# A hybrid mixer block on one core: scores over 128 rows, another order of the branches, weights of the last stage a tile ahead

## The chip, the core and the metric

The kernel runs on one core of a Trainium2 chip. TensorE (PE in the rows; PEld is its weight load) multiplies matrices, VectorE (DVE) works on whole tiles, ScalarE (ACT) computes functions and copies, and SyncE (SP) issues most transfers; each engine takes its instructions in the order in which the program holds them. The metric is the device time of one execution in microseconds (us), lower is better.

## What is computed

One block over 1024 tokens of 1024 features. Four branches of width 256 are computed from a normalized input, each is multiplied by its own matrix and gated, and their sum goes through an output matrix; a gated FFN and a last gated projection follow.

```python
h = rmsnorm(x, g_mix)
(a_b, a_c, a_x, q, k, v, s_u, s_v, c_val, c_gate) = split(h @ w_in, 10)   # 256 features each
y_a = a_b * causal_dwconv(a_c * a_x, conv_a)          # short convolution, 3 taps
y_b = dilated_attention(q, k, v)                      # 4 heads of 64, three window groups in one softmax
y_c = spatial_gating(s_u, s_v, sgu_ln_g, sgu_ln_b, sgu_w, sgu_b)
y_d = conformer_conv(c_val, c_gate, conf_dw, conf_ln_g, conf_ln_b)        # 31 taps
merged = sum(sigmoid(h @ w_merge_gate[br]) * (branches[br] @ w_branch[br]) for br in range(4))
x = x + merged @ w_out
f_gate, f_up = split(rmsnorm(x, g_ffn) @ w_ffn_in, 2)                     # hidden 2816
x = x + (silu(f_gate) * f_up) @ w_ffn_out
x = x + sigmoid(rmsnorm(x, g_ple) @ w_ple_gate) * (p @ w_ple_proj)
return rmsnorm(x, g_final)
```

## The kernel before

Features lie on the 128 partitions, tokens in the free dimension. A product of F32 values is made of three matmuls: each operand is split into a rounded F32R part (`h`, "hi", a ScalarE cast) and the rest (`l`, "lo", a VectorE subtraction), and `mm_k` adds hi·hi, lo·hi and hi·lo. The large square products (branch gates, `gt`; FFN, `fg`/`fo`) use seven block products instead of eight (`pair`); its seven weights `p0` to `p6` are sums of blocks, split like the others.

The program is written as one pass; a scheduler fixes the order on each engine when the program is built, and tile pools decide when a buffer can be taken again: T and M (large tiles), W (raw weights, 3 buffers), WS (2), WP (a hi and a lo pool of 4 each). The stages in time: projections to 99.6 us; attention to 222 us; spatial gating, conformer and short convolution to 320 us; the gates and branches to 717 us; output matrix and FFN to 1449 us; the last stage to the end.

**Attention.** `qk(ct)` makes queries and keys of one column tile of 128 features, two heads of 64. For head h it writes `qs` (query hi in the head's 64 rows, query lo in the other 64) and `kd` (key hi in both halves), so that one matmul over 128 rows gives hi·hi + lo·hi. The third product takes `kl`, the keys' lo parts of both heads in one tile, over the head's 64 rows alone (L396). `attend` loops over 8 blocks of 128 queries and 2 heads, 32 steps in all: the scores `sc` go into one PSUM buffer (L395, L396, in pieces of up to 512 keys, so 48 pairs), VectorE adds the mask and takes the minimum (L400), ScalarE exponentiates (L402), PE transposes (L409), ScalarE copies the transposed block (L410), PE multiplies by the values (L415). Between these PE has projections of other branches (`pj`, `sp`), and VectorE has the 31 taps of the conformer convolution (L332).

**Branches.** For each branch in `ORDER`, `load_parts` reads its output `y` back from DRAM (`yda` to `ydd`, written there by `spill`) and splits it; then for four pairs of column tiles `pair` computes the gates, and the branch's product `br` is gated and added to `mg`. The short convolution (`short_conv`, branch 0) is the last branch that is computed before this loop, in six steps; between its steps `gate_operands` prepares the normalized input for the gates. ScalarE copies partial gate sums out of PSUM (`gt00n<-gt00u`, L580).

**Last stage.** `PIECES` are 768 and 256 tokens; for each output tile m of 8, `pg` is the gate's product (weights `wpg`, 1024 deep) and `pq` the projection's (weights `wpp`, 256 deep). Tiles 4 to 7 of `wpg` are kept split for the second piece, the others are read and split again. Then VectorE scales (L891), ScalarE takes the sigmoid (L892), VectorE multiplies and adds (L893, L895), ScalarE squares for the last norm (L899, L906). The finished first piece is scaled meanwhile by VectorE (L858) and written out. At the end `rsqrt_col` sums the squares (`fin1ss`, PE) and takes a square root on ScalarE (L215).

Of the kernel before, what the change touches and what calls it, by code (L numbers as in the profile page):

```python
# [8 lines left out]
F32 = mybir.dt.float32  # L9
F32R = mybir.dt.float32r  # L10
AF = mybir.ActivationFunctionType
# [12 lines left out]
NEG = 3.0e38  # L24
CHUNKS = ((0, 4), (4, 7))
SINGLE = ((7, 8, 9), (10,))
ORDER = (0, 1, 2, 3)
PIECES = ((0, 768), (768, 256))


# [9 lines left out]
def mixers_kernel(ctx, tc, xT, pT, vec, mask, sgu_ln, sgu_wT, sgu_b, w_in, w_tok, w_gate, w_br, w_out,  # L40
# [27 lines left out]
    def M(name, dt=F32, w=S):  # L68
        return mp.tile([P, w], dt, tag="m", name=name, padded_shape=[P, S], bufs=8)
# [1 line left out]
    def W(name, w=S):  # L71
        return wp.tile([P, w], F32, tag="wr", name=name, padded_shape=[P, S], bufs=3)

    def WS(name, w=512):
        return wp.tile([P, w], F32, tag="sw", name=name, padded_shape=[P, 512], bufs=2)

    def WP(name):
        return (wp.tile([P, 512], F32R, tag="wh", name=name + "h", bufs=4),
# [274 lines left out]

    def qk(ct):

        qs, kd = [], []
        kl = None
        for nm, i in (("q", 6 + ct), ("k", 8 + ct)):
            ps = proj_tile(i)
            t = T(f"{nm}{ct}")  # L360
            if nm == "q":
                nc.vector.scalar_tensor_tensor(t, ps, -(64.0 ** -0.5), rs, ALU.mult, ALU.mult)
                for h in range(2):
                    a, b = slice(h * 64, h * 64 + 64), slice(64 - h * 64, 128 - h * 64)
                    d = M(f"qs{ct}{h}", F32R)
                    nc.scalar.copy(d[a, :], t[a, :])
                    nc.vector.tensor_sub(d[b, :], t[a, :], d[a, :].bitcast(F32))
                    qs.append(d)
            else:
                nc.vector.tensor_mul(t, ps, rs)  # L370
                kl = M(f"kl{ct}", F32R)
                for h in range(2):
                    a, b = slice(h * 64, h * 64 + 64), slice(64 - h * 64, 128 - h * 64)
                    d = M(f"kd{ct}{h}", F32R)
                    nc.scalar.copy(d[a, :], t[a, :])
                    nc.scalar.copy(d[b, :], t[a, :])
                    nc.vector.tensor_sub(kl[a, :], t[a, :], d[a, :].bitcast(F32))
                    kd.append(d)
        return qs, kd, kl

    yb = [T(f"yb{ct}") for ct in range(2)]
# [3 lines left out]
    def attend(ct, qs, kd, kl):  # L385
        for b in range(NB):
            L = (b + 1) * P
            rl = sm.tile([P, 2, 64], F32, tag="rl", name=f"rl{ct}{b}", bufs=2)
            for h in range(2):
                a = slice(h * 64, h * 64 + 64)  # L390
                sc = banks.pools["s"].tile([P, S], F32, tag="s", name=f"sc{ct}{b}{h}", bufs=1)
                q = qs[h][:, b * P:(b + 1) * P]
                for c in range(0, L, 512):
                    n = min(512, L - c)
                    nc.tensor.matmul(sc[:, c:c + n], q, kd[h][:, c:c + n], start=True, stop=False)  # L395
                    nc.tensor.matmul(sc[:, c:c + n], q[a, :], kl[a, c:c + n], start=False, stop=True)  # L396
                pr, pt = prs[h], pts[h]
                nm = sm.tile([P, 1], F32, tag="nm", name=f"nm{ct}{b}{h}")
                ls = sm.tile([P, 1], F32, tag="ls", name=f"ls{ct}{b}{h}")
# [231 lines left out]
        yield  # L631

    for n, _ in enumerate(step for ct in range(2) for step in short_conv(ct)):
        if 1 <= n <= 4:
            gate_operands(n - 1)


    banks.close()
# [145 lines left out]

    ws = {(i, c): load_single(i, c) for i, c in ((SINGLE[0][0], 0), (SINGLE[0][0], S))}
    acts = [single_operands(i) for i in SINGLE[0][:2]]
    for ci, (i0, i1) in enumerate(CHUNKS):
        n = i1 - i0

# [38 lines left out]
        for m in range(0, KD, 2):  # L828
            for k, h, ps, t in pair(f"fo{ci}{m}", raws if m == 0 else load_two(m), n):
                x = x2[m + k][:, h * 512:h * 512 + 512]  # L830
                if ci == 1 and m == 6 and (k, h) == (1, 0):
                    wpg0, wpp0 = load_w("wpg00", w_pg[0]), load_w("wpp00", w_pp[0], 256)
                nc.vector.tensor_add(x, x, t)
                nc.vector.tensor_add(x, ps, x)
                if ci == 1 and m == 6 and ready:
                    i = ready.pop(0)
                    n3.add(i, x2[i])
            ready += [m, m + 1]
            while ci == 1 and m != 4 and ready:
                i = ready.pop(0)  # L840
                n3.add(i, x2[i])
# [3 lines left out]
    banks = Banks(True)  # L845


    kept = {}
    late = []

    def finish(ci, c0, H, acc):
# [8 lines left out]

        return [norm] + [lambda m=m: out(m) for m in range(KD)]

    ORD2 = (4, 5, 6, 7, 0, 1, 2, 3)
    xg = []
    steps = []
    for ci, (c0, H) in enumerate(PIECES):
        acc = T(f"oacc{ci}", F32, H)
        for m in (tuple(range(KD)), ORD2)[ci]:
            if m in kept:
                w = kept[m]  # L870
            elif m >= 4:
                raw = W(f"wpg{m}r")
                nc.sync.dma_start(raw, w_pg[m])
                hi, lo = parts(f"wpg{m}", raw).both
                w = kept[m] = [(hi[:, c:c + P], lo[:, c:c + P]) for c in range(0, S, P)]
            else:
                w = load_w(f"wpg{ci}{m}", w_pg[m]) if ci or m else wpg0
            wq = load_w(f"wpp{ci}{m}", w_pp[m], 256) if ci or m else wpp0
            if H > 512:
                pg, po = G(f"pg{ci}{m}"), G(f"pq{ci}{m}")  # L880
            else:
# [5 lines left out]
                         [(c, min(c + 512, c0 + H)) for c in range(c0, c0 + H, 512)], c0)  # L887
            if ci == m == 0:
                r3 = n3.rstd()
            t = T(f"pt{ci}{m}", F32, H)  # L890
            nc.vector.tensor_mul(t, pg[:, :H], r3[:, c0:c0 + H])  # L891
            nc.scalar.activation(t, t, AF.Sigmoid)  # L892
            nc.vector.tensor_mul(t, t, po[:, :H])  # L893
            xs = x2[m][:, c0:c0 + H]
            nc.vector.tensor_add(xs, xs, t)  # L895
            if m == 4 * ci:
# [111 lines left out]
```

## Time and profile before

| | us |
|---|---|
| median of 3 runs | 1584.57 |
| lowest, highest | 1583.59, 1586.0 |
| profiled execution | 1587.8 |
| span of that execution | 1585.9 |
| PE busy in it | 1565.9 (99%) |
| DVE busy in it | 1186.1 (75%) |
| ACT busy in it | 681.2 (43%) |

The rows come from the profiled execution, which took 3.2 us more than the median; 1.9 us of its time lie outside the span. Its mean granted clock of TensorE was 0.996 of full speed. "Busy" of PE counts overlapping instructions once. In the rows, "idle before" is the engine's idle time just ahead of an instruction, and the arrow names what ended it.

### The profile page before, as it was taken

What the parts mean: (1) busy time and instruction counts of PE and PEld (TensorE: products, weight loads), DVE (VectorE), ACT (ScalarE), POOL (GpSimd) and SP (SyncE); (2) the same over time, 40 slices, a digit from 0 to 9 for tenths busy, and PEclk for the clock granted to TensorE, in tenths of its full rate; (3) what the DMA queues carried; (4) which work ended last, traced back from release to release, by engine and by line L of the source; (5) the groups of instructions that cost most, each with busy time, mean ns of one, the idle gap of its engine ahead of it and who ended that gap; (6) DMA issues with size and microseconds to landing.
All of it is one profiled execution on the core that took longest, in us unless ns stands there. A gap on an engine that the chain in (4) does not pass through costs nothing.

```text
span 1585.9 us, 19898 instructions
## 1 busy us (share of the span) xinstructions
PE 1565.9 (99%) x7542; PEld 1291.5 (81%) x7542; DVE 1186.1 (75%) x1885; ACT 681.2 (43%) x1171; POOL 1.2 (0%) x6
## 2 busy tenths in 40 slices
PE   9999999999999999999999999999999999999996
PEld 7976788878888888888888888888888888877886
DVE  7988885766677777777678888888777666688556
ACT  6325553333334334354554444444444123255334
POOL 0000000000000000000000000000000000000000
PEclk9999999999999999999999999999999999999998
DMA  6110233121212112123414444444337971812214
GB/s 226 55 41 14 70 120 120 67 80 47 93 36 91 54 47 93 51 74 123 144 66 147 147 149 157 146 146 151 115 106 279 380 282 54 325 63 74 67 47 143
DMA packets 56224, 186.03 MB, mean 117 GB/s; under 512 B 6336, under 2 KB 9664, under 8 KB 56128
## 3 DMA queue, kind: packets, MB, share of 16 engines
q1 hardware_dynamic: 45504, 148.52, 27.8%
q10 hardware_dynamic: 10624, 36.23, 5.7%
q8 instruction: 59, 0.97, 0.3%
q14 instruction: 37, 0.30, 0.1%
HBM read 138.07 MB, written 46.66 MB: 116 GB/s over the span
## 4 chain that ended last, share of the span: by engine, by line
PE 96%; DVE 2%; DMA 1%; ACT 1%; issue 0%; SPq 0%; DVEq 0%; ACTq 0%
PE pj L153 11%; PE wo L153 5%; PE fs L153 5%; PE br L153 5%; PE pg L153 5%; PE po L415 1%; PE pq L153 1%; PE sc L396 1%; PE ptp L409 1%; PE sc L395 1%; PE sp L319 1%; PE sp L317 1%; PE fg0u L572 1%; PE fo00u L572 1%; PE fo06u L572 1%; PE fo04u L572 1%
## 5 line engine op out<-in xcount | busy, mean ns | idle before, releaser
L332 DVE SCALAR_TENSOR_TENSOR cacc<-cy,vs,cacc 128x1023 f32<-128x1023 f32 (+29 forms) x60 | 76.1, 1269 | 0.5
L783 DVE TENSOR_TENSOR x<-fs,x 128x512 f32<-128x512 f32 x64 | 43.9, 690 | 26.1 <-PE fs L153 25.5
L410 ACT COPY pt<-ptp 128x512 f32<-128x512 f32 (+3 forms) x48 | 21.8, 481 | 35.5 <-PE ptp L409 35.5
L400 DVE CUSTOM_DVE_ANT_0 pr<-sc,maskt 128x128 f32<-128x128 f32 (+7 forms) x32 | 24.1, 753 | 9.2 <-PE sc L396 8.8
L153 PE MATMUL pj<-n1p,w1h 128*128 128x512 f32 x96 | 27.6, 408 | 1.2 <-ACT n1p L193 1.2
L402 ACT ACTIVATE pr<-pr,nm 128x128 f32<-128x128 f32 (+7 forms) x32 | 24.9, 779 | 5.5 <-DVE nm L400 5.3
L891 DVE TENSOR_TENSOR pt<-pg,n3r 128x768 f32<-128x768 f32 (+1 forms) x16 | 11.0, 689 | 21.4 <-PE pg L153 20.9
L153 PEld LDWEIGHTS pj<-n1p,w1h 128*128 128x128 f32 x96 | 18.8, 197 | 6.0 <-ACT n1p L193 2.0
L415 PE MATMUL po<-pt,vt 128*64 128x128 f32 x288 | 22.7, 279 | 0.2
L689 DVE TENSOR_TENSOR xr<-wo,xr 128x512 f32<-128x512 f32 x16 | 11.0, 688 | 15.6 <-PE wo L153 15.6
L409 PE MATMUL ptp<-ident,pr 128*128 128x128 f32 x144 | 22.2, 276 | 0.0
L892 ACT ACTIVATE pt<-pt 128x768 f32<-128x768 f32 (+1 forms) x16 | 10.1, 631 | 26.9 <-DVE pt L891 26.9
L415 PEld LDWEIGHTS po<-pt,vt 128*64 128x64 f32 x288 | 16.9, 136 | 5.8 <-issue 2.8
L396 PE MATMUL sc<-kl,qs 64*128 64x512 f32 (+3 forms) x48 | 21.0, 438 | 0.0
L690 ACT ACTIVATE x1g<-xr,vs 128x512 f32<-128x512 f32 x16 | 11.6, 724 | 18.0 <-DVE xr L689 18.0
L409 PEld LDWEIGHTS ptp<-ident,pr 128*128 128x128 f32 x144 | 16.6, 140 | 3.1 <-ACT rb L420 1.0
L395 PE MATMUL sc<-kd,qs 128*128 128x512 f32 (+3 forms) x48 | 18.7, 390 | 0.1
L396 PEld LDWEIGHTS sc<-kl,qs 64*128 64x128 f32 x48 | 8.8, 183 | 10.0 <-issue 8.6
L899 ACT ACTIVATE pt<-x 128x768 f32<-128x768 f32 (+1 forms) x13 | 8.4, 646 | 16.6 <-DVE x L895 16.6
L153 PE MATMUL pj<-n1p,w1l 128*128 128x512 f32 x48 | 15.4, 400 | 0.0
L893 DVE TENSOR_TENSOR pt<-pt,pq 128x768 f32<-128x768 f32 (+1 forms) x16 | 10.9, 685 | 5.4 <-ACT pt L892 2.9
L693 DVE TENSOR_TENSOR ssq<-ssq,sq 128x512 f32<-128x512 f32 x14 | 9.6, 689 | 6.4 <-ACT sq L691 6.4
(4328 smaller groups left out, 5256.7 us busy)
## 6 DMA issues: line engine op xcount, KB each, us to landing
hl<-fd SPq DMA_DIRECT2D x65, 512.0 KB, 10.1
fd<-ho0i ACTq DMA_DIRECT2D x11, 512.0 KB, 2.6
fd<-ho1i ACTq DMA_DIRECT2D x11, 512.0 KB, 4.8
fd<-ho2i ACTq DMA_DIRECT2D x11, 512.0 KB, 4.1
fd<-ho3i ACTq DMA_DIRECT2D x11, 512.0 KB, 2.6
xg<-in_xT SPq DMA_DIRECT2D x8, 512.0 KB, 4.0
xr<-in_xT SPq DMA_DIRECT2D x8, 512.0 KB, 5.1
x1d<-xr SPq DMA_DIRECT2D x8, 512.0 KB, 2.9
```

What stands on the lines that cost most here:

```text
L153: nc.tensor.matmul(ps[:, c - off:e - off], w[n], act.part(p, c, e), start=(first and i == 0), stop=(last and i == 2))
L317: nc.tensor.matmul(o, ah, wh, start=(k == 0), stop=False)
L332: nc.vector.scalar_tensor_tensor(acc[:, d:], y[:, :S - d], wj, acc[:, d:], ALU.mult, ALU.add)
L395: nc.tensor.matmul(sc[:, c:c + n], q, kd[h][:, c:c + n], start=True, stop=False)
L396: nc.tensor.matmul(sc[:, c:c + n], q[a, :], kl[a, c:c + n], start=False, stop=True)
L400: nc.vector.tensor_tensor_reduce(out=pr[:, :L], in0=sc[:, :L], in1=maskt[:, S - L:], scale=1.0, scalar=NEG, op0=ALU.add, op1=ALU.min, accu ...
L402: nc.scalar.activation(pr[:, :L], pr[:, :L], AF.Exp, bias=nm, scale=-1.0, accum_out=ls)
L409: nc.tensor.transpose(pa[:, j * P:(j + 1) * P], pr[:, c + j * P:c + (j + 1) * P], ident)
L410: nc.scalar.copy(pt[:, c:c + n], pa[:, :n])
L415: nc.tensor.matmul(po[h * 64:h * 64 + 64, :P], vtok[j // 4][:, hc:hc + 64], pts[h][:, j * P:(j + 1) * P], start=(j == 0), stop=(j == b))
L572: nc.tensor.matmul(ps, ww, x[:, c:c + 512], start=(first and i == 0 and j == 0), stop=(i == n - 1 and j == 2), skip_group_check=not first)
L783: nc.vector.tensor_add(x, pm, x)
```

## The change

Four edits, in neutral words:

1. In `qk`, each head gets a tile `kl` of its own whose 128 rows hold the key's lo part twice (one more ScalarE cast of 64x1024 for each head and column tile, four in all); `attend`'s second matmul then runs over 128 rows, and adds the lo·lo term too.
2. `ORDER` becomes (1, 2, 3, 0): attention's branch is merged first, the short convolution's last. `gate_operands` moves one step of `short_conv` earlier.
3. The last stage's weights are read and split by `gate_weights` for the next tile of `WALK`, behind the current tile's matmuls; the parts of `wpp` go into one WS tile instead of a pair of WP buffers. The first tile's weights are asked for at the same place in the FFN's code as before; on VectorE the split of `wpp00` then stands ahead of that of the FFN's last weights, `fo16p6`, and before it stood behind it, ahead of the additions of L833 and L834.
4. Behind the last sigmoid a square root of one column is taken, which loads the table of the square root there; the last tile's product goes to a new tile `ptlast`.

```diff
-ORDER = (0, 1, 2, 3)
+ORDER = (1, 2, 3, 0)
...
-    def WS(name, w=512):
-        return wp.tile([P, w], F32, tag="sw", name=name, padded_shape=[P, 512], bufs=2)
+    def WS(name, w=512, dt=F32):
+        return wp.tile([P, w], dt, tag="sw", name=name, padded_shape=[P, 512], bufs=2)
...
-                kl = M(f"kl{ct}", F32R)
                 for h in range(2):
                     a, b = slice(h * 64, h * 64 + 64), slice(64 - h * 64, 128 - h * 64)
-                    d = M(f"kd{ct}{h}", F32R)
+                    d, e = M(f"kd{ct}{h}", F32R), T(f"kl{ct}{h}", F32R)
                     nc.scalar.copy(d[a, :], t[a, :])
                     nc.scalar.copy(d[b, :], t[a, :])
-                    nc.vector.tensor_sub(kl[a, :], t[a, :], d[a, :].bitcast(F32))
+                    nc.vector.tensor_sub(e[a, :], t[a, :], d[a, :].bitcast(F32))
+                    nc.scalar.copy(e[b, :], e[a, :].bitcast(F32))
                     kd.append(d)
+                    kl.append(e)
...
-                    nc.tensor.matmul(sc[:, c:c + n], q[a, :], kl[a, c:c + n], start=False, stop=True)
+                    nc.tensor.matmul(sc[:, c:c + n], q, kl[h][:, c:c + n], start=False, stop=True)
...
     for n, _ in enumerate(step for ct in range(2) for step in short_conv(ct)):
-        if 1 <= n <= 4:
-            gate_operands(n - 1)
+        if n < 4:
+            gate_operands(n)
...
+    WALK = [(0, m) for m in range(KD)] + [(1, m) for m in ORD2]
+
+    def gate_weights(ci, m):
+        if m in kept:
+            w = kept[m]
+        else:
+            raw = W(f"wpg{ci}{m}r")
+            nc.sync.dma_start(raw, w_pg[m])
+            if m >= 4:
+                hi, lo = parts(f"wpg{m}", raw).both
+                w = kept[m] = [(hi[:, c:c + P], lo[:, c:c + P]) for c in range(0, S, P)]
+            else:
+                w = w_parts(f"wpg{ci}{m}", raw, S)
+        raw = W(f"wpp{ci}{m}r", 256)
+        nc.sync.dma_start(raw, w_pp[m])
+        q = WS(f"wpp{ci}{m}", dt=F32R)
+        split(q[:, :256], q[:, 256:], raw)
+        return w, [(q[:, c:c + P], q[:, 256 + c:256 + c + P]) for c in (0, P)]
...
-                    wpg0, wpp0 = load_w("wpg00", w_pg[0]), load_w("wpp00", w_pp[0], 256)
+                    weights = gate_weights(0, 0)
...
+            n = WALK.index((ci, m)) + 1
+            if n < len(WALK):
+                weights = gate_weights(*WALK[n])
             t = T(f"pt{ci}{m}", F32, H)
             nc.vector.tensor_mul(t, pg[:, :H], r3[:, c0:c0 + H])
             nc.scalar.activation(t, t, AF.Sigmoid)
-            nc.vector.tensor_mul(t, t, po[:, :H])
+            if ci == 1 and m == ORD2[-1]:
+                sqrt = sm.tile([P, 1], F32, tag="nm", name="sqrt")
+                nc.scalar.activation(sqrt, t[:, 0:1], AF.Sqrt)
+                s = t
+                t = T("ptlast", F32, H)
+                nc.vector.tensor_mul(t, s, po[:, :H])
+            else:
+                nc.vector.tensor_mul(t, t, po[:, :H])
```

The scheduler's order at three places. First ScalarE at the start of the branches, before the change; `gt00` is branch 0's first gate pair, `y01` the second half of branch 0's output read back from DRAM.

```order
L112 CAST gt00p2h<-gt00s_2923 128x512
L112 CAST gt00p3h<-gt00ra 128x512
L112 CAST gt00p4h<-gt00s_2963 128x512
L112 CAST gt00p5h<-gt00s_2923 128x512
L112 CAST gt00p6h<-gt00rb 128x512
L112 CAST y01h<-y01l 128x1024
L580 COPY gt00n_2884<-gt00u 128x512
L583 COPY gt00n_2884<-gt00q 128x512
L648 ACT_TABLE_LOAD
```

The same place after the change; `gt01` is branch 1's first gate pair, `y10` and `y11` are the two halves of branch 1's output.

```order
L112 CAST y10h<-y10l 128x1024
L112 CAST gt01p2h<-gt01s_2929 128x512
L112 CAST y11h<-y11l 128x1024
L112 CAST gt01p3h<-gt01ra 128x512
L112 CAST gt01p4h<-gt01s_2969 128x512
L579 COPY gt01n_2890<-gt01u 128x512
L112 CAST gt01p5h<-gt01s_2929 128x512
L582 COPY gt01n_2890<-gt01q 128x512
L112 CAST gt01p6h<-gt01rb 128x512
L586 COPY gt01n_2947<-gt01u 128x512
L112 CAST wb010h<-wb01r 128x512
```

The two casts of the branch's output have moved from just ahead of the copy `gt00n<-gt00u` to ahead of the split of `p3`, and between the split of `p4` and the copy nothing stands any more.

Second, VectorE in the last stage's second piece, before: the scaling of the finished first piece (L858, 768 wide) among the second piece's own steps (256 wide), and the split of `wpg10`'s second half, `wpg10512l`.

```order
L895 TENSOR_TENSOR x_10219<-x_10219,pt_12873 128x256
L891 TENSOR_TENSOR pt_12923<-pg_12891,n3r 128x256
L858 SCALAR_TENSOR_TENSOR x_10195<-x_10195,vs,fin0r 128x768
L891 TENSOR_TENSOR pt_12971<-pg_12939,n3r 128x256
L900 TENSOR_TENSOR oacc_12760<-oacc_12760,pt_12873 128x256
L858 SCALAR_TENSOR_TENSOR x_10217<-x_10217,vs,fin0r 128x768
L893 TENSOR_TENSOR pt_12923<-pt_12923,pq_12892 128x256
L893 TENSOR_TENSOR pt_12971<-pt_12971,pq_12940 128x256
L895 TENSOR_TENSOR x_10221<-x_10221,pt_12923 128x256
L895 TENSOR_TENSOR x_10223<-x_10223,pt_12971 128x256
L113 TENSOR_TENSOR wpg10512l<-wpg10r,wpg10512h 128x512
L900 TENSOR_TENSOR oacc_12760<-oacc_12760,pt_12923 128x256
```

After the change (L858 is L877 there, L891 to L900 are L903 to L919), from the diagonal `fin0dg` of the first piece's norm on, which is ahead of the scalings in both:

```order
L228 TENSOR_TENSOR fin0dg_12823<-ident,fin0srp 128x768
L113 TENSOR_TENSOR wpg100l<-wpg10r,wpg100h 128x512
L903 TENSOR_TENSOR pt_12874<-pg_12837,n3r 128x256
L113 TENSOR_TENSOR wpg10512l<-wpg10r,wpg10512h 128x512
L877 SCALAR_TENSOR_TENSOR x_10195<-x_10195,vs,fin0r 128x768
L877 SCALAR_TENSOR_TENSOR x_10197<-x_10197,vs,fin0r 128x768
L912 TENSOR_TENSOR pt_12874<-pt_12874,pq_12838 128x256
L877 SCALAR_TENSOR_TENSOR x_10199<-x_10199,vs,fin0r 128x768
L914 TENSOR_TENSOR x_10225<-x_10225,pt_12874 128x256
L113 TENSOR_TENSOR wpp_12920<-wpp17r,wpp_12920 128x256
```

The split `wpg10512l` has moved from behind the scalings to ahead of the first of them, and the split of that weight's first half stands just before it.

Third, ScalarE at the very end, before, from the square of the tile before the last on:

```order
L899 ACTIVATE pt_13146<-x_10193 128x256
L907 ACTIVATE xg_13036<-x_10193,vs 128x256
L892 ACTIVATE pt_13204<-pt_13204 128x256
L906 ACTIVATE pt_13204<-x_10195 128x256
L907 ACTIVATE xg_13036<-x_10195,vs 128x256
L215 ACT_TABLE_LOAD
L215 ACTIVATE fin1sr<-fin1ss,epst 128x2
```

After the change (L892 is L904, L899 and L906 are L918 and L925, L907 is L926):

```order
L904 ACTIVATE pt_13152<-pt_13152 128x256
L904 ACTIVATE pt_13194<-pt_13194 128x256
L918 ACTIVATE pt_13152<-x_10199 128x256
L926 ACTIVATE xg_13044<-x_10199,vs 128x256
L907 ACT_TABLE_LOAD
L907 ACTIVATE sqrt<-pt_13194 128x1
L925 ACTIVATE ptlast<-x_10201 128x256
L926 ACTIVATE xg_13044<-x_10201,vs 128x256
L215 ACTIVATE fin1sr<-fin1ss,epst 128x2
```

The table load has moved from behind the last tile's square and product to ahead of them; the square and product of the tile before stand between the last sigmoid and it.

## Rows read from the trace of the kernel before

**Rows 1.** The page's first part: busy us, share of the span, instructions.

```profile
PE 1565.9 (99%) x7542; PEld 1291.5 (81%) x7542; DVE 1186.1 (75%) x1885; ACT 681.2 (43%) x1171; POOL 1.2 (0%) x6
```

**Rows 2.** Timeline of PE: start us, us, engine, line, operation.

```profile
168.50 0.28 PE L317 MATMUL sp<-sp01h,n1p 128*128 128x256 f32 x1
168.62 0.28 PE L395 MATMUL sc<-kd,qs 128*128 128x256 f32 x1
168.83 0.38 PE L396 MATMUL sc<-kl,qs 64*128 64x256 f32 x1
169.14 0.38 PE L318 MATMUL sp<-sp01l,n1p 128*128 128x256 f32 x1
169.36 0.28 PE L319 MATMUL sp<-sp01h,n1p 128*128 128x256 f32 x1
169.48 0.27 PE L409 MATMUL ptp<-ident,pr 128*128 128x128 f32 x1
```

**Rows 3.** Weight loads of the scores: duration ns min/median/max, first and last start.

```profile
L396 PEld LDWEIGHTS sc<-kl,qs x48: 182/183/183, 99.9 to 214.4; 64*128 64x128 f32 x48
```

**Rows 4.** Windows over attention's two column tiles, their sum: busy us by engine.

```profile
sum 122.40, PE 122.13 PEld 89.51 DVE 97.28 ACT 68.34 POOL 0.69; mean PE 61.07 PEld 44.76 DVE 48.64 ACT 34.17 POOL 0.35
```

**Rows 5.** VectorE's groups in attention: busy, mean ns, idle before and releaser.

```profile
L332 DVE SCALAR_TENSOR_TENSOR cacc<-cy,vs,cacc 128x997 f32<-128x997 f32 (+29 forms) x34 | 43.1, 1270 | 0.1
L400 DVE CUSTOM_DVE_ANT_0 pr<-sc,maskt 128x128 f32<-128x128 f32 (+7 forms) x32 | 24.1, 753 | 9.2 <-PE sc L396 8.8
...
L421 DVE TENSOR_TENSOR yb<-rb,po 128x128 f32<-128x128 f32 x15 | 4.3, 285 | 7.0 <-ACT rb L420 6.9
```

**Rows 6.** The tile of the doubled keys: one of its casts.

```profile
L376 ACT CAST kd<-k x4: 1044/1046/1051, 57.9 to 164.9; 64x1024 fp32r<-64x1024 f32 x4
```

**Rows 7.** Timeline at the first branch's start, several engines.

```profile
327.64 0.33 SPq L169 DMA_DIRECT2D y01l<-yda  x1
...
331.76 1.04 ACT L112 CAST y01h<-y01l 128x1024 fp32r<-128x1024 f32 x1 [2.93 <-DMA y01l<-yda]
...
333.34 0.73 PE L572 MATMUL gt00u<-go2i,gt00p2h 128*128 128x512 f32 x2 [2.32 <-ACT gt00n L580]
```

**Rows 8.** Windows over the first branch's opening; PEclk is the granted clock.

```profile
320.08:344.40 24.32, 21.52 (x86) 16.67 (x84) 11.50 (x17) 8.94 (x14) 0.00 (x0) 0.93 0.31 98
334.60:338.10 3.50, 3.50 (x10) 2.71 (x9) 0.76 (x2) 1.44 (x3) 0.00 (x0) 0.51 0.00 0
```

**Rows 9.** PE's waits: us in total, times, longest.

```profile
PE pg L153 <- DVE wpg10512l L113: 0.8, 1, 0.8
PE pg L153 <- DVE x L834: 0.7, 1, 0.7
PE pq L153 <- ACT wpp110h L112: 0.6, 1, 0.6
PE pq L153 <- DVE wpp000l L113: 0.5, 1, 0.5
...
PE pq L153 <- ACT wpg010h L112: 0.5, 1, 0.5
...
PE pg L153 <- DVE wpg130l L113: 0.2, 1, 0.2
```

**Rows 10.** Timeline of VectorE in the last 256 tokens' part.

```profile
1550.55 1.95 DVE L858 SCALAR_TENSOR_TENSOR x<-x,vs,fin0r 128x768 f32<-128x768 f32 x2 [2.39 <-ACT fin0r L237]
...
1558.44 0.69 DVE L113 TENSOR_TENSOR wpg10512l<-wpg10r,wpg10512h 128x512 fp32r<-128x512 f32 x1
```

**Rows 11.** Window over that part.

```profile
1550.50:1574.80 24.30, 21.50 (x169) 20.50 (x168) 22.56 (x45) 13.73 (x32) 0.00 (x0) 1.00 0.54 190
```

**Rows 12.** Timeline of ScalarE at the end.

```profile
1573.48 0.42 ACT L892 ACTIVATE pt<-pt 128x256 f32<-128x256 f32 x1 [0.81 <-DVE pt L891]
...
1575.68 1.28 ACT L215 ACT_TABLE_LOAD   x1
1576.98 0.26 ACT L215 ACTIVATE fin1sr<-fin1ss,epst 128x2 f32<-128x2 f32 x1
```

More of the change, by code (lines that the diff above doesn't have):

```diff
@@ L354, in qk @@
     def qk(ct):
-        qs, kd = [], []
-        kl = None
+        qs, kd, kl = [], [], []
         for nm, i in (("q", 6 + ct), ("k", 8 + ct)):
@@ L389, in attend @@
             for h in range(2):
-                a = slice(h * 64, h * 64 + 64)
                 sc = banks.pools["s"].tile([P, S], F32, tag="s", name=f"sc{ct}{b}{h}", bufs=1)
@@ L786, in mixers_kernel @@
     acts = [single_operands(i) for i in SINGLE[0][:2]]
+    kept = {}
+    ORD2 = (4, 5, 6, 7, 0, 1, 2, 3)
+    WALK = [(0, m) for m in range(KD)] + [(1, m) for m in ORD2]
[15 more added lines that the diff above has]
+        return w, [(q[:, c:c + P], q[:, 256 + c:256 + c + P]) for c in (0, P)]
     for ci, (i0, i1) in enumerate(CHUNKS):
@@ L845, in mixers_kernel @@
     banks = Banks(True)
-    kept = {}
     late = []
@@ L861, in finish @@
         return [norm] + [lambda m=m: out(m) for m in range(KD)]
-    ORD2 = (4, 5, 6, 7, 0, 1, 2, 3)
     xg = []
@@ L868, in mixers_kernel @@
         for m in (tuple(range(KD)), ORD2)[ci]:
[L869 to L878, printed above, removed]
+            w, wq = weights
             if H > 512:
```

## The prediction

> **What bounds the kernel now.** I read the page first: PE is busy 1565.9 of 1585.9 us [rows 1], so only what shortens PE's own work, or the 20.0 us in which it has none, can pay. Next come PE's waits. They are short and few; the two ends of the change's places stand in them: 2.3 us for a copy at the branches' start [rows 7], and four waits at the last stage's weights [rows 9]. Last I read the timeline inside attention, since a busy PE is not PE at its peak: there the starts of neighbouring matmuls show what one costs [rows 2], the windows what the other engines do meanwhile [rows 4], and VectorE's groups what it waits for [rows 5].
>
> **Scores over 128 rows.** Matmuls 256 wide over 128 rows start 0.12 us apart (168.50 to 168.62, and 169.36 to 169.48). Around the one of 64 rows the starts are 0.21, 0.31 and 0.22 apart [rows 2]: 0.09 more to go into it, 0.19 more to leave it, 0.10 more on the matmul after that, 0.38 in all. There are 48 such visits [rows 3]. In 16 steps (blocks 4 to 7, two heads, two column tiles) two pairs may follow each other and share the trailing 0.10, so I count 48 x 0.28 + 32 x 0.10 = 16.6 us of PE time. That the columns number 256 here and up to 512 elsewhere I neglect: the extra is time between shapes, not time per column. As the new form is one that the rows show at 0.12, PE's own saving is firm, if the 64 rows are the cause.
>
> Whether the clock on the wall gets it is VectorE's affair. PE is busy 122.13 of these 122.40 us [rows 4], without waits, because projections fill it. VectorE is busy 97.28, idle 25.1. With 16.6 us less the stage would be 105.8 us and VectorE 92% busy, in a fixed order with 34 taps of 1.27 us each between its short steps [rows 5]. Of its idle time 8.8 us were ended by the score matmul itself and 6.9 by the copy of the transposed reciprocals, which again follows PE [rows 5]. A faster PE takes away the former, and the latter about by half, for half of that chain is ScalarE's. The rest are latencies of ScalarE and of transfers, which stay. So VectorE lets the stage shrink by about 8.8 + 3.5 = 12.3 us. The bounds are 16.6 (filler covers all new waits) and 5 (VectorE keeps four fifths of its idle time). I take 12.3, which lies nearer to the upper one, because PE has shown no wait in the whole stage. The four added casts are 1.05 us each [rows 6], 4.2 us on a ScalarE that is busy 68.34 of 122.40 [rows 4]; two lie long before attention, two make the second column tile's first scores about 1 us later, while spatial projections are there for PE. Without that cover they would cost 2.1 us.
>
> The Trainium skill speaks against this part: "TensorE: Matmul & The Clock Gate", in "The mechanism" of its Part 3 on packing small matmuls, says that a weight load overlaps with running matmuls only when its row group differs. By that each second matmul would now expose its load, as an estimate from the row of 0.183 us [rows 3] 48 x 0.183 = 8.8 us, and 7.8 of the 16.6 would be left. The trace does not agree: a score matmul over 128 rows starts 0.12 us behind another of 128 rows [rows 2], less than one load takes.
>
> **Short convolution's branch last.** Its second half was written to DRAM as the last thing before the branches. The reload is issued at 327.64, and the cast of y01 comes at 331.76, after 2.93 us in which ScalarE had nothing else that it could do; the copy that frees PE's sums is queued behind that cast, and PE stands still for 2.32 us until 333.34 [rows 7]. From 320.08 to 344.40 PE is busy 21.52 of 24.32, so 2.80 are lost. From 334.60, right after the standstill, 3.50 us run at a granted clock of 0.51, which is the 1.2 GHz level [rows 8]; the same work at full clock takes about 1.8, another 1.7. Together 4.5; a restarting matmul adds some tenths, and I take 5.0, bounds 4.5 and 5.5. After the change the first branch is attention's, whose output went to DRAM some 100 us earlier, and between the split of p4 and the copy nothing stands on ScalarE any more. The short convolution's reload then comes three branches later, on a SP queue with hundreds of us to spare. `gate_operands` one step earlier puts the same two reads and casts of a step where PE has projections; I count it at nothing. If the gate operands came late instead, PE would wait for them in that place, one cast of about 1 us each.
>
> **Weights a tile ahead.** In the second piece PE waits 0.8 for wpg10's second half, 0.6 for wpp11, and twice 0.2 (one of the two rows shown) [rows 9], 1.8 together. The window holds 24.30 us with PE busy 21.50, thus 2.80 lost, and VectorE busy 22.56 [rows 11]. VectorE stood idle 2.39 us until 1550.55, and split wpg10's second half only at 1558.44 behind four scalings of the first piece [rows 10]; the new order has both halves in that idle time. That removes one split of 0.69 from VectorE's full stretch besides its idle 1.74: 2.4 us. Bounds: 1.2 (VectorE, 93% busy, keeps its own gaps) and 2.8 (all of PE's loss). I take 2.4, as the two engines' limits lie together there.
>
> At the stage's opening PE waits 0.7 for L834 [rows 9]. The earlier split of wpp00 lets that addition come sooner by the length of one 256-wide split, and the two other waits of 0.5 each [rows 9] collapse into this one; between 0 and 0.7 I take 0.35. The idle time of PE becomes one piece instead of three, and a piece of 2.3 us was followed by the lower clock [rows 7, 8]; at 1 in 5, times 1.7, that takes 0.35 back.
>
> **Square root ahead.** Before, the sigmoid starts at 1573.48, the load of 1.28 at 1575.68 and the root at 1576.98, 3.50 behind the sigmoid [rows 12]. The load was exposed by about 1.3. In the new order the square and the scaled copy of the tile before come between sigmoid and load, so last sigmoid 0.3, square and copy 0.8, load and root 1.5, last square and copy 0.8, then the sum of squares through PE and the wait for it: about 3.9. That loses 0.4; bounds are a gain of 0.5 (the two are done before the sigmoid) and a loss of 0.8. The last stage then gives 2.4 + 0.35 - 0.35 - 0.4 = 2.0, with bounds 0 and 3.5.
>
> "ScalarE: Activation LUTs", under "What ACT_TABLE_LOAD costs", in the Trainium skill adds a drain of about 1.38 us to each load. The root starts 0.02 us after the load's end [rows 12], so no drain shows behind it. With one the moved load would delay the last square by 2.7 instead of 1.3, as an estimate from that page, and the sum would be 1.4 us worse.
>
> **Sum.** 12.3 + 5.0 + 2.0 = 19.3 us off the profiled 1587.8 gives 1568.5. That execution was 3.2 above the median of 1584.57, so I forecast 1565.3, rounded 1565. With the bounds of each term (8 in attention as the worst that I still call this case, 4.5, 0.5; and 16.6, 5.5, 3.5) its own range is 1559 to 1572.
>
> **Rivals.** (a) VectorE is the bound in attention: it keeps most of its idle time, since a 1.27 us tap stands ahead of the next reduction and the only score buffer stays taken. For: 92% busy in a fixed order. Against: 8.8 us of its idle time waited for PE alone. Attention gives 5: 5 + 5 + 2 = 12, 1572.6. Chance 0.18. (b) The stall at the branches only moves: the copy or split that follows is late by other means, as ScalarE and VectorE also split seven weights there. Against: the row names the reload alone. 12.3 + 2.0: 1570.3. Chance 0.08. (c) The weight loads stay exposed because both matmuls now use the same rows: each second score matmul starts 0.3 behind the first, 48 x 0.183 [rows 3] = 8.8 us come back, and of the other 7.8, by VectorE's share 12.3 / 16.6, attention gives 5.8: 1571.8. Against: the 0.12 between other pairs of 128 rows [rows 2]. Chance 0.05. (d) The 64 rows are not the cause, the starts stay 0.2 to 0.3 apart (for instance because a product into the same sums follows), and the casts cost their 4.2: 5 + 2 - 4.2 = 2.8 gained, 1581.8. Against: the matmul after it, with other sums, also starts late. Chance 0.04. (e) Slower: PE runs out of independent work in the 32 steps of attention, and waits for each step's reduction, exponential and copies, which a shorter filler no longer covers. From a mean wait of (16.6 + 7 + 3.2) / 32 = 0.84 us a step it is slower by over 0.2%, the 3.2 us that a measurement of this kernel can about tell from no change. One tap of 1.27 us in the way at each step would do it: at 1.0 us, 32 - 23.6 = 8.4 lost, 1593. Against: no wait of PE there now, and the tap is already there. Chance 0.03.
>
> The forecast has 0.62. Faster are it and (a) to (c), 0.93; (d) is the same, 0.04; (e) slower, 0.03. The range 1557 to 1575 leaves out (d), (e), a third of (a), where attention gives less than 3, and 5 in 100 of the forecast beyond its bounds: about 18 in 100.
>
> **What would show it.** Right: the second score matmul starts 0.12 (256 wide) behind the first and the next 0.12 behind it; VectorE is over 90% busy in attention, and PE has small new waits on the reduction's and the copies' results; no wait at the first gates and a granted clock of 1.00 through 320 to 345; no waits for wpg10, wpp11 and wpg13, one of about 2 us for L834's successor at the opening; the root 3.9 us behind the last sigmoid. Wrong: many PE waits above 0.8 us in attention, starts still 0.2 to 0.3 apart, a lower clock in attention or at the opening, or a wait for y1's cast in the place of y0's.

## The result and the profile after

The changed kernel takes 1566.51 us (median of 4 runs, 1564.67 to 1568.01) against 1585.28 for the kernel before beside it; the ratio is 0.9883, 95% interval 0.9871 to 0.9895, that is 18.6 us less (16.6 to 20.5). The forecast was 1565. Its profiled execution took 1567.4 us.

The page's first part has PE still at 99% of a shorter span; against [rows 1] its busy time fell by 18.3 us, all but 1.9 of what the span lost.

```profile
PE 1547.6 (99%) x7542; PEld 1288.2 (82%) x7542; DVE 1184.2 (76%) x1885; ACT 685.1 (44%) x1176; POOL 1.7 (0%) x6
```

The timeline of PE in attention, at the same kind of place as [rows 2]: a pair of score matmuls (L394, L395) between projections.

```profile
163.18 0.28 PE L318 MATMUL sp<-sp02l,n1p 128*128 128x256 f32 x1
163.30 0.28 PE L394 MATMUL sc<-kd,qs 128*128 128x256 f32 x1
163.42 0.28 PE L395 MATMUL sc<-kl,qs 128*128 128x256 f32 x1
163.54 0.28 PE L319 MATMUL sp<-sp02h,n1p 128*128 128x256 f32 x1
163.66 0.28 PE L317 MATMUL sp<-sp02h,n1p 128*128 128x256 f32 x1
```

The weight loads of the second score matmul, from the tile's own view of the changed kernel (minimum, median and maximum in ns):

```profile
L395 PEld LDWEIGHTS sc<-kl,qs x48: 186/188/192, 100.7 to 203.1; 128*128 128x128 f32 x48
```

Every start is 0.12 behind the one before it, into the pair, within it and out of it. At [rows 2] the same four steps took 0.12, 0.21, 0.31 and 0.22.

The weight loads themselves differ too. First two at the place of [rows 2] in the kernel before, that of the second score matmul and that of the matmul behind it, then the second score matmul's in the changed kernel:

```profile
168.83 0.18 PEld L396 LDWEIGHTS sc<-kl,qs 64*128 64x128 f32 x1
169.13 0.19 PEld L318 LDWEIGHTS sp<-sp01l,n1p 128*128 128x128 f32 x1
```
```profile
163.30 0.19 PEld L395 LDWEIGHTS sc<-kl,qs 128*128 128x128 f32 x1
```

In the kernel before, both loads start together with the matmul that uses them (168.83 and 169.14); in the changed kernel the load starts with the matmul ahead of it (163.30), 0.12 before its own. That holds for the whole stage: of the 48 loads of the second score matmul none starts ahead of its own matmul in the kernel before, and 47 do in the changed kernel.

The windows from the first score matmul to the first matmul of the branch gates, the kernel before first, then the changed one (columns as in [rows 4], then the granted clock, the DMA engines' busy share and GB/s).

```profile
99.78:320.08 220.30, 220.03 (x1306) 169.52 (x1304) 169.74 (x323) 101.61 (x199) 0.69 (x1) 1.00 0.22 73
```
```profile
100.66:307.55 206.89, 205.57 (x1306) 167.40 (x1304) 170.84 (x325) 104.44 (x202) 1.19 (x1) 1.00 0.24 80
```

The same PE work takes 220.30 and 206.89: 13.4 less. PE's busy time fell by 14.5, and its time without work grew from 0.27 to 1.32.

VectorE's groups in attention, which answer to [rows 5] (L400 is L399 here, L403 is L402, L421 is L420):

```profile
L399 DVE CUSTOM_DVE_ANT_0 pr<-sc,maskt 128x128 f32<-128x128 f32 (+7 forms) x32 | 24.0, 749 | 5.8 <-PE sc L395 5.6
...
L402 DVE RECIPROCAL ls<-ls 128x1 f32<-128x1 f32 x32 | 5.1, 159 | 1.5 <-ACT pr L401 1.2
L420 DVE TENSOR_TENSOR yb<-rb,po 128x128 f32<-128x128 f32 x16 | 4.6, 285 | 4.6 <-ACT rb L419 4.6
```

The idle time that scores ended fell from 8.8 to 5.6, that for the reciprocals from 6.9 to 4.6. About 64% of the former stayed, where I had it vanish. A third wait, for the exponential's sums (`pr`), which I had counted among those that stay, fell from 4.3 to 1.2; its line in the kernel before:

```profile
L403 DVE RECIPROCAL ls<-ls 128x1 f32<-128x1 f32 x32 | 5.0, 159 | 4.4 <-ACT pr L402 4.3
```

PE's waits in the whole changed kernel, which answer to [rows 7, 9]:

```profile
PE pg L153 <- DVE x L854: 1.3, 1, 1.3
...
PE fin1ss L212 <- DVE oacc L919: 1.2, 1, 1.2
...
PE pg L153 <- DVE wpg130l L113: 0.8, 1, 0.8
...
PE ptp L408 <- ACT pr L401: 0.5, 2, 0.3
...
PE sc L395 <- ACT kl L376: 0.4, 1, 0.4
```

The wait at the first gates, those for wpg10 and for wpp11 are gone. That for wpg13 is not: it was twice 0.2 and is 0.8, since VectorE splits the first half only at 1548.00, behind a product that waited 0.71 for a sigmoid. New are small ones in attention (0.5 for the exponential, 0.4 for the doubled key part) and one of 1.2 at the end. The window that answers to [rows 8], the opening of the branches:

```profile
307.30:335.00 27.70, 27.70 (x124) 22.92 (x123) 18.19 (x27) 11.38 (x19) 0.00 (x0) 1.00 0.23 70
```

PE is busy through all of it at a granted clock of 1.00, where [rows 8] has 2.80 us lost and 3.50 us at 0.51.

In the last stage PE comes to the first gate product as follows; the last FFN matmul starts at 1431.46.

```profile
1431.46 0.39 PE L571 MATMUL fo16e<-hl,fo16p6l 128*128 128x512 f32 x1
1432.19 0.62 PE L153 MATMUL pq<-pp0h,wpp 128*128 128x512 f32 x2 [0.34 <-DVE x L854]
...
1435.88 0.47 PE L153 MATMUL pg<-n3h,wpg000h 128*128 128x512 f32 x1 [1.30 <-DVE x L854]
```

One wait of 0.34 and one of 1.30 replaced three (0.5, 0.5, 0.7 [rows 9]); I had looked for a single one of about 2. VectorE's timeline, which answers to [rows 10], has the split of wpg10's second half ahead of the scalings:

```profile
1529.45 0.68 DVE L113 TENSOR_TENSOR wpg10512l<-wpg10r,wpg10512h 128x512 fp32r<-128x512 f32 x1
1531.27 1.02 DVE L877 SCALAR_TENSOR_TENSOR x<-x,vs,fin0r 128x768 f32<-128x768 f32 x1 [1.14 <-ACT fin0r L237]
```

ScalarE's timeline at the end, which answers to [rows 12] (L904 is the last sigmoid, L925 the last square, L215 the root):

```profile
1552.25 0.42 ACT L904 ACTIVATE pt<-pt 128x256 f32<-128x256 f32 x1 [1.17 <-DVE pt L903]
...
1553.41 1.28 ACT L907 ACT_TABLE_LOAD   x1
...
1554.82 0.40 ACT L925 ACTIVATE ptlast<-x 128x256 f32<-128x256 f32 x1
...
1556.70 0.26 ACT L215 ACTIVATE fin1sr<-fin1ss,epst 128x2 f32<-128x2 f32 x1 [1.09 <-PE fin1ss L212]
```

The root comes 4.45 us behind the last sigmoid, where it came 3.50 behind it. It no longer waits for its table but for the sums on PE (L212), which start as follows, two to a row:

```profile
1555.27 0.55 PE L212 MATMUL fin1ss<-onesf,ptlast 128*128 128x1 f32 x2 [1.38 <-ACT ptlast L925]
1555.68 0.56 PE L212 MATMUL fin1ss<-onesf,oacc 128*128 128x1 f32 x2
```

### The profile page after: what moved, and what is told of

Its sections match the earlier page's. It is cut to its first block, busy times and chain, and to the rows that moved or that the text cites. A ratio compares the mean times of both kernels' runs of the same rounds, so it can differ in the third digit from the quotient of the medians.

```text
span 1565.7 us, 19884 instructions
## 1 busy us (share of the span) xinstructions
PE 1547.6 (99%) x7542; PEld 1288.2 (82%) x7542; DVE 1184.2 (76%) x1885; ACT 685.1 (44%) x1176; POOL 1.7 (0%) x6
## 4 chain that ended last, share of the span: by engine, by line
PE 96%; DVE 1%; ACT 1%; DMA 1%; issue 0%; SPq 0%; DVEq 0%; ACTq 0%
PE pj L153 11%; PE wo L153 6%; PE fs L153 6%; PE br L153 6%; PE pg L153 5%; PE po L414 1%; PE ptp L408 1%; PE pq L153 1%; PE sc L394 1%; PE fg0u L571 1%; PE fo00u L571 1%; PE fu2u L571 1%; PE sc L395 1%; PE fo06u L571 1%; PE fo04u L571 1%; PE fo02u L571 1%
## 5 line engine op out<-in xcount | busy, mean ns | idle before, releaser
L903 DVE TENSOR_TENSOR pt<-pg,n3r 128x768 f32<-128x768 f32 (+1 forms) x16 | 11.0, 686 | 24.1 <-PE pg L153 23.6
L399 DVE CUSTOM_DVE_ANT_0 pr<-sc,maskt 128x128 f32<-128x128 f32 (+7 forms) x32 | 24.0, 749 | 5.8 <-PE sc L395 5.6
L904 ACT ACTIVATE pt<-pt 128x768 f32<-128x768 f32 (+1 forms) x16 | 10.1, 631 | 33.9 <-DVE pt L903 33.9
L689 ACT ACTIVATE x1g<-xr,vs 128x512 f32<-128x512 f32 x16 | 11.6, 724 | 18.0 <-DVE xr L688 18.0
L394 PE MATMUL sc<-kd,qs 128*128 128x512 f32 (+3 forms) x48 | 18.0, 375 | 0.0
L395 PE MATMUL sc<-kl,qs 128*128 128x512 f32 (+3 forms) x48 | 16.6, 353 | 0.4 <-ACT kl L376 0.4
L153 PE MATMUL pj<-n1p,w1l 128*128 128x512 f32 x48 | 15.9, 411 | 0.0
L918 ACT ACTIVATE pt<-x 128x768 f32<-128x768 f32 (+1 forms) x13 | 8.4, 647 | 16.9 <-DVE x L914 16.9
L919 DVE TENSOR_TENSOR oacc<-oacc,pt 128x768 f32<-128x768 f32 (+1 forms) x13 | 9.2, 708 | 5.5 <-ACT pt L918 5.5
```

The lines of the kernel that those rows point to most:

```text
L153: nc.tensor.matmul(ps[:, c - off:e - off], w[n], act.part(p, c, e), start=(first and i == 0), stop=(last and i == 2))
L395: nc.tensor.matmul(sc[:, c:c + n], q, kl[h][:, c:c + n], start=False, stop=True)
L399: nc.vector.tensor_tensor_reduce(out=pr[:, :L], in0=sc[:, :L], in1=maskt[:, S - L:], scale=1.0, scalar=NEG, op0=ALU.add, op1=ALU.min, accu ...
L689: nc.scalar.activation(xg[n][:, c:c + 512], t, AF.Copy, scale=vs[:, V_GFFN + m:V_GFFN + m + 1])
```

## The experiments

**e1: scores over 128 rows alone.** The kernel before with edit 1, of which this is the last line:

```diff
...
-                    nc.tensor.matmul(sc[:, c:c + n], q[a, :], kl[a, c:c + n], start=False, stop=True)
+                    nc.tensor.matmul(sc[:, c:c + n], q, kl[h][:, c:c + n], start=False, stop=True)
```

> The kernel before with the scores over 128 rows alone (edit 1). If the extra time between shapes is the cause, the starts around the second score matmul fall to 0.12 us at 256 columns, and the time by about 12.3 to 13: 1572 to 1573. Rival: part of what attention gained in the changed kernel comes from another order of its filler that the other edits brought; then this alone gives 8 or less, 1577 or more. Rival of late casts: PE waits of over 2 us in all for kl.

Measured: ratio 0.9914 (0.9900 to 0.9927), 13.6 us less (11.6 to 15.9), median 1572.01. Its window from the first score matmul to the first gate matmul:

```profile
98.20:305.19 206.99, 205.59 (x1305) 167.41 (x1304) 168.73 (x324) 103.56 (x201) 0.79 (x1) 1.00 0.24 78
```

It takes 206.99, the changed kernel 206.89. So edit 1 alone makes all of attention's gain, and the earlier gate operands of edit 2 neither add to it nor take from it (with edit 2 alone the stage takes 220.31). The starts around the 256-wide pair are 0.12 apart here as well. The rival of late casts falls: PE waits for `kl` once, 0.4 us.

**e2: the branches' order alone.** The kernel before with `ORDER = (1, 2, 3, 0)` and `gate_operands(n)` for n under 4:

```diff
-ORDER = (0, 1, 2, 3)
+ORDER = (1, 2, 3, 0)
...
```

> The kernel before with the branches' order (1, 2, 3, 0) and the earlier gate operands alone (edit 2). Forecast: the wait of 2.32 us at the first gates and the low clock behind it are gone, 5.0 us gained, 1580. Rival: the stall only moves to another load or split, gain under 1.5, 1583.5 or more.

Measured: ratio 0.9973 (0.9962 to 0.9985), 4.3 us less (2.4 to 6.0), median 1582.12. No wait at the first gates is in its list. The rival falls.

**e3: the last stage's weights a tile ahead, alone.** The kernel before with edit 3, in part:

```diff
...
+            n = WALK.index((ci, m)) + 1
+            if n < len(WALK):
+                weights = gate_weights(*WALK[n])
...
```

> The kernel before with the last stage's weights a tile ahead alone (edit 3). By the forecast's terms 2.4 at the second piece and 0.0 to 0.35 at the opening: 2.4 to 2.8 gained, 1582. The changed kernel's trace says more, 0.3 at the opening and 3.4 in the pieces, 3.7 in all: 1581. Rival: VectorE keeps its gaps, 1.2 gained, 1583.5.

Measured: ratio 0.9988 (0.9977 to 0.9998), 1.9 us less (0.3 to 3.6), median 1584.11. The forecast's 2.4 lies inside, and so does the rival's 1.2: the whole time can't tell them apart. The 3.7 read from the two traces lies just outside; why it was too much stands below, on the pace. The trace decides against the rival: in the second piece the weights ahead gain 2.3 (below).

**e4: the square root ahead, alone.** The kernel before with edit 4, in part:

```diff
...
+                sqrt = sm.tile([P, 1], F32, tag="nm", name="sqrt")
+                nc.scalar.activation(sqrt, t[:, 0:1], AF.Sqrt)
...
```

> The kernel before with the square root taken ahead alone (edit 4). By the forecast the load delays the last square: the root comes 3.9 us behind the last sigmoid in place of 3.50, 0.4 lost. By the changed kernel's trace it comes 4.45 behind, 0.95 lost. Rival: here the square and copy of the tile before are done before the last sigmoid, so the load starts at once, and the root comes about 3.0 to 3.4 behind it, 0.1 to 0.5 gained. All of it lies below what the timing can tell; the trace decides.

Measured: ratio 1.0001 (0.9992 to 1.0010), no difference. Its ScalarE timeline at the end (L892 the last sigmoid, L913 the last square, L215 the root):

```profile
1571.46 0.42 ACT L892 ACTIVATE pt<-pt 128x256 f32<-128x256 f32 x1 [0.82 <-DVE pt L891]
1571.89 1.28 ACT L895 ACT_TABLE_LOAD   x1
...
1573.29 0.40 ACT L913 ACTIVATE ptlast<-x 128x256 f32<-128x256 f32 x1
...
1574.61 0.26 ACT L215 ACTIVATE fin1sr<-fin1ss,epst 128x2 f32<-128x2 f32 x1 [0.52 <-PE fin1ss L212]
```

The load starts right behind the sigmoid, and the root comes 3.15 behind it, 0.35 sooner than in [rows 12]. The rival was right here: by itself the edit brings the root a little forward, by less than the whole time can show.

**e5: the second score matmul over 64 rows, twice.**

```diff
-                    nc.tensor.matmul(sc[:, c:c + n], q[a, :], kl[a, c:c + n], start=False, stop=True)
+                    nc.tensor.matmul(sc[:, c:c + n], q[a, :], kl[a, c:c + n], start=False, stop=False)
+                    nc.tensor.matmul(sc[:, c:c + n], q[a, :], kl[a, c:c + n], start=False, stop=True)
```

> The kernel before with its second score matmul over 64 rows issued twice in a row, so that the keys' lo part enters twice. Theory: changing between 128 and 64 rows costs, a matmul over 64 rows by itself does not; the second of the two starts 0.12 us behind the first at 256 columns and 0.227 at 512, the extra on entering and leaving stays once, and the 48 added matmuls cost about 8 us: 1593. Rival: each matmul over 64 rows is slow by itself; it starts 0.31 behind at 256 columns and 0.425 at 512, about 17 us: 1602.

Measured: ratio 1.0065 (1.0048 to 1.0082), 10.3 us more (7.6 to 13.0), median 1595.0. A group of three and the next pair's first, 512 wide, on its PE timeline (L396 and L397 are the two of 64 rows):

```profile
206.72 0.39 PE L395 MATMUL sc<-kd,qs 128*128 128x512 f32 x1
207.04 0.50 PE L396 MATMUL sc<-kl,qs 64*128 64x512 f32 x1
207.38 0.39 PE L397 MATMUL sc<-kl,qs 64*128 64x512 f32 x1
207.70 0.44 PE L395 MATMUL sc<-kd,qs 128*128 128x384 f32 x1
```

and the same place in the kernel before, with one of 64 rows:

```profile
199.90 0.39 PE L395 MATMUL sc<-kd,qs 128*128 128x512 f32 x1
200.22 0.49 PE L396 MATMUL sc<-kl,qs 64*128 64x512 f32 x1
200.64 0.44 PE L395 MATMUL sc<-kd,qs 128*128 128x384 f32 x1
```

The time is that of the theory within its interval, not the rival's 17. The starts show more than either said: the step from 64 rows to 64 rows takes 0.34, not the 0.227 that I expected nor the rival's 0.425, and the step out to 128 rows then falls from 0.42 to 0.32. So the theory's step was wrong: a matmul over 64 rows behind another of 64 is not as cheap as one among full ones. But the extra of a visit is spread over more matmuls and hardly grows: the whole stage took 230.32 in place of 220.30, 0.21 for each added matmul, where the theory's 8 us are 0.17.

**e6 and e7: fewer taps on VectorE, without and with edit 1.** Both leave out 40 of the 60 multiply-adds of the conformer convolution, so what they compute is not the block:

```diff
-    for j in reversed(range(CK - 1)):
+    for j in reversed(range(CK - 11, CK - 1)):
```

> The kernel before with 10 of the 30 added taps of the conformer convolution in each column tile; 40 of its 60 multiply-adds on VectorE, about 50 us of its work, are left out. PE shows no wait in attention, so both theories expect the same time within 3 us of the kernel before, 1582 to 1586. It is the base for the next run.

> The same with the scores over 128 rows (edit 1) besides. If VectorE's load held attention back in the changed kernel, the edit is worth PE's full saving here, 16 to 18 us against the run without it. Rival: VectorE's taps held nothing back, and what is missing of the 16.6 goes to latencies and to other neighbours of the score matmuls: 12 to 14 us as with all taps.

Measured: e6 1585.32, ratio 0.9998 (0.9985 to 1.0012); e7 1571.29, ratio 0.9915 (0.9900 to 0.9929); between their medians 14.0 us. The windows from the first score to the first gate matmul, e6 and then e7:

```profile
101.59:321.68 220.09, 219.77 (x1306) 170.00 (x1304) 145.55 (x300) 101.57 (x199) 0.63 (x1) 1.00 0.22 73
```
```profile
99.57:306.76 207.19, 206.83 (x1306) 167.71 (x1305) 144.01 (x300) 102.86 (x201) 0.63 (x1) 1.00 0.24 78
```

Edit 1 gives 12.9 us here, against 13.3 with all taps, although VectorE is busy 144.01 instead of 168.73 of about 207 and PE lost only 0.36, where it lost 1.40 in e1. At most that difference of 1.0 us can be laid to the taps; the gain did not grow by it. So VectorE did not hold the gain back, and the rival of this run is right.

**e8: the changed kernel without the square root ahead.** Edits 1 to 3.

```diff
-                nc.scalar.activation(sqrt, t[:, 0:1], AF.Sqrt)
...
+            nc.vector.tensor_mul(t, t, po[:, :H])
```

> The changed kernel without the square root ahead (edits 1 to 3). The kernel with edit 3 alone has the reciprocals' product on PE 4.86 us behind the last projection matmul, the changed kernel 5.60, the kernel before 4.53. Theory: in the new order the table load stands ahead of the last square and costs; without it 4.86 again, 0.7 less than the changed kernel, and 1566. Rival: the lateness is VectorE's, and the place of the load does not matter: 5.4 or more.

Measured: ratio 0.9878 (0.9862 to 0.9895), median 1566.82. Its ScalarE timeline at the end (L918 the last square):

```profile
1554.71 0.42 ACT L904 ACTIVATE pt<-pt 128x256 f32<-128x256 f32 x1 [1.18 <-DVE pt L903]
...
1556.29 0.42 ACT L918 ACTIVATE pt<-x 128x256 f32<-128x256 f32 x1 [0.43 <-DVE x L907]
...
1557.12 1.28 ACT L215 ACT_TABLE_LOAD   x1
1558.41 0.26 ACT L215 ACTIVATE fin1sr<-fin1ss,epst 128x2 f32<-128x2 f32 x1
```

The root comes 3.70 behind the last sigmoid, 0.75 sooner than with the load ahead; the reciprocals' product on PE follows the last projection matmul by 4.85. That is the theory's figure; the whole time cannot tell it. But the load's place is not all of the 0.75: about 0.5 of it is a lower clock in the changed kernel's execution (below, on the square root).

**e9: the changed kernel with the last square on VectorE.**

```diff
                 if m == ORD2[-1]:
-                    nc.scalar.activation(t, xs, AF.Square)
+                    nc.vector.tensor_mul(t, xs, xs)
```

> The changed kernel with the last tile's square computed on VectorE, right behind its addition, in place of ScalarE. The load is then beside it: VectorE ends the square about 0.7 us behind the addition, so the sums start 1.1 us sooner than in the changed kernel and the product of the reciprocals follows the last projection matmul by about 4.5 us in place of 5.60; 1565. Rival: PE's idle time before the sums slows them, and the root is not sooner: 5.3 or more.

Measured: ratio 0.9877 (0.9862 to 0.9892), median 1566.24. Its ScalarE timeline at the end:

```profile
1552.60 0.42 ACT L904 ACTIVATE pt<-pt 128x256 f32<-128x256 f32 x1 [1.17 <-DVE pt L903]
...
1553.77 1.28 ACT L907 ACT_TABLE_LOAD   x1
...
1555.57 0.24 ACT L215 ACTIVATE fin1sr<-fin1ss,epst 128x2 f32<-128x2 f32 x1
```

The sums on PE start closer together than in the changed kernel:

```profile
1554.66 0.38 PE L212 MATMUL fin1ss<-onesf,ptlast 128*128 128x1 f32 x2 [0.41 <-DVE ptlast L925]
1554.90 0.36 PE L212 MATMUL fin1ss<-onesf,oacc 128*128 128x1 f32 x2
```

The root is 2.97 behind the sigmoid, 1.48 sooner than in the changed kernel, and the product follows the last projection matmul by 4.10 in place of 5.60. The rival falls. Of the 1.48, too, about 0.5 is the clock. This has the shortest end of all, and it is the version to keep, but a gain of 1.5 us is below what this timing tells from none.

## Why the prediction was right, and where it was not

**Sum.** Forecast 19.3 us; measured 18.6. The three parts alone measured 13.6, 4.3 and 1.9 and the fourth nothing, 19.8 together, against terms of 12.3, 5.0 and 2.0.

**Attention, 12.3: the size was right, its second step was not.** That the 64 rows cost the time is shown: e1 alone takes it away, the starts fall to 0.12, and by e5 it is paid for a visit, hardly more for a second matmul in it. What goes with it the traces show as well: at a change between 128 and 64 rows no weight load starts ahead of its own matmul (none of 48 on the way in, none of 48 on the way out), and between two score matmuls of 128 rows 47 of 48 do. That the late load is what costs is read from this and was not tested by itself. Rivals (c) and (d) fall with the same rows: a second score matmul over 128 rows starts 0.12 behind the first, with its load ahead; the exposed load that (c) feared in the new form is the old form's.

But 12.3 came from 16.6 of PE's own saving, cut down because VectorE would only follow by so much. e6 and e7 refute the cut, and rival (a) with it: with two thirds of the taps gone the edit was worth no more. So 16.6 was too much and the cut was made for a wrong reason; that the two errors met near the measured 13.4 is luck. PE's own saving was the smaller number: 14.4 us of busy time in e1, 0.30 for each of 48 visits, where I counted 0.346 from one place, and 1.1 went to new waits, which leaves 13.3. That one place was dear: its 0.10 on the matmul after the visit does not recur everywhere. Where a transpose follows a pair 512 wide, as at 4 of the 48 places, the two steps took 0.41 and 0.43 before and take 0.32 and 0.29 now, 0.23 less and not 0.38. What is open is why e7, with 0.36 us of PE's time without work, gained 12.9 and not 14.4; its order of filler is another one. I looked for VectorE over 90% busy in attention; it was 88% (97.41 of 110.60). Rival (e), PE out of filler, had its place right (new waits of PE are there) and its size far off: 1.1 us over 32 steps is 0.03 a step, not 0.84.

The rule that a weight load overlaps only when the row group differs, from "TensorE: Matmul & The Clock Gate" in the Trainium skill ("The mechanism" in Part 3), would have left 7.8 of 16.6. The traces of the changed kernel and of e1 don't agree with it: loads of 0.188 us lie beside matmuls 0.12 apart. Where the rows did differ, in the kernel before, the loads were late.

**Branches, 5.0: the mechanism was right, the size came from a dear execution.** The wait and the low clock are gone [rows 7, 8], nothing took their place (rival (b)), and e2 alone gained 4.3. By the starts of their first matmuls, the part from the gates to the output matrix took 391.68 in e2 and in the changed kernel, 396.96 in the profiled execution of before, so 5.28 there. But the stall is no constant. The six other executions with the old order took 394.44 to 397.17, with waits of 1.4 to 2.5, as the reload landed sooner or later (3.2 to 4.4 us behind its issue). And the lower clock came in two of seven only, those with waits of 2.3 and 2.5; e6, with 2.4, kept a granted clock of 1.00. The windows of 17 us from the same place in e4 (a wait of 2.5) and in e1 (1.4):

```profile
326.80:343.80 17.00, 13.99 (x52) 10.42 (x52) 6.32 (x9) 7.62 (x12) 0.00 (x0) 0.90 0.22 65
```
```profile
313.10:330.10 17.00, 15.09 (x64) 11.57 (x63) 9.07 (x14) 9.14 (x14) 0.00 (x0) 1.00 0.20 64
```

The seven executions of the old order give 2.8 to 5.5 and 3.8 in the mean. My bounds of 4.5 and 5.5 were bounds of the reading, not of the thing.

**Weights a tile ahead, 2.4 and 0.35: right in size, though one wait stayed.** From the last FFN matmul to the first gate product it took 4.71 before and 4.42 after, 0.29 gained; the clock did not fall, so the 0.35 set aside for that were not needed. From the last product of the first piece's weights to the end of the projections the seven executions of the old code took 18.4 to 19.0, 18.6 in the mean, e3 and the changed kernel 16.3: 2.3. That no wait for wpg13 would be left was wrong; it takes 0.8 of these 16.3.

**Square root ahead, 0.4 lost: right but for the clock.** The forecast's 3.9 behind the last sigmoid was 4.45. I had the order right, and the parts ahead of the last square: it starts 2.57 behind the sigmoid, where I had 2.6. What came late is the next step, the sums on PE. In the changed kernel each of the six starts about 0.21 behind the one before it, in e9 0.11 to 0.13. The window over them in the changed kernel:

```profile
1555.00:1557.00 2.00, 1.40 (x6) 1.31 (x6) 0.00 (x1) 0.88 (x3) 0.00 (x0) 0.59 0.00 0
```

The granted clock is 0.59 in it: it falls to 0.5, the 1.2 GHz level, at 1555.34. Over the same work in e9 (1554.6 to 1556.6) it is 1.00. From the first of the six sums to the root it takes 1.43 in the changed kernel and 0.91 in e9; as an estimate from these two, the root would have come at full clock 0.52 sooner, 3.93 behind the sigmoid, which is the forecast's figure. In all eleven executions the clock falls to that level 2.2 to 5.4 us after the start of the last projection matmul, ahead of the end of the sums in three of them (e1, e3 and the changed kernel). It is not the idle time alone that decides: in e4 PE stood idle for 1.95 us ahead of the sums, and they ran at 1.00. So by itself the edit brings the root 0.35 forward (e4); behind edit 3 it puts it off by 0.75 in these executions (e8 against the changed kernel), and by about 0.2 at equal clock, since PE's work ends earlier there, VectorE and ScalarE are behind it, and the square and copy of the tile before stand between the last sigmoid and the load. The drain of 1.38 us that "ScalarE: Activation LUTs" of the Trainium skill ("What ACT_TABLE_LOAD costs") adds to a load shows in none of these ends: in e4 the load of 1.28 at 1571.89 is followed by the next ScalarE work within 0.1 us.

## What to carry to other kernels

A matmul over half the rows in the midst of full ones is not a cheaper one: look at the distance of starts on both sides of it and at where the weight loads start, and fill the other half with something harmless. Take a stall's price from several executions if it hangs on a transfer's landing, since its size and the clock behind it vary. A table load moved ahead pays only if nothing late is queued around it: look at which instructions the order puts ahead of it and behind it. Before two short stretches of two executions are compared, look at the granted clock in both.

## What was not expected of the hardware

The tiles of the last stage's first piece run at one of two paces in an execution, at a granted clock of 1.00 in both: 10.40 us a tile (the changed kernel, e2, e4, e5, e7) or 10.60 (before, e1, e3, e6, e8, e9), though their instructions are the same. Over the piece that is about 1.2 us. Why, no run here shows. The trace of the changed kernel fell on the fast one and that of before on the slow one, and this made the 3.7 of e3's expectation out of 2.5. The first score matmul, too, came between 98.2 and 102.0 us in these traces, with the same work ahead of it: part of each difference of two whole spans is the start's.

The product with the values (`po`), a matmul over 128 rows with 64 columns of weights, has late loads as the 64 rows had: at none of its edges in attention does a load start ahead of its own matmul. From the first score to the first gate matmul of the changed kernel PE still goes into it 27 times and out of it 27 times; as an estimate from the starts, against those between equal shapes, each change costs about 0.14 us, 7.4 in all. No run here takes them away.
